# Tile offsets, parameter loads, scan outputs and two products in turn: one change in a four-part kernel

## The chip, the cores and the metric

The kernel runs on one core of a Trainium2 chip. The metric is device time in microseconds (us) per execution, the median of several runs. A profile is one further execution, recorded by the hardware profiler. Its spans are measured from the first to the last instruction of that execution.

## The reference

The input `x` has 512 tokens of width 1024, in fp32. Four mixers follow each other, each on a normalised copy of the residual `h`, and each adds its result to `h`:

```python
h = h + gated_delta_and_pool_mixer(rms_norm(h)) @ w_out              # first block
u = rms_norm(h); h = h + square(relu(u @ w_up)) @ w_down             # MLP, 1024 -> 4096 -> 1024
h = rms_norm(h)
h = h + nsa(rms_norm(h))     # attention: compressed, selected and window keys, gates, 16 heads of 64
h = h + s5(rms_norm(h))      # state space layer
return rms_norm(h)

# s5:
u, z = split(rms_norm(h) @ w_in, 2)                  # 2 x 1024 channels
y = scan(a, bb @ u) with (c_re, c_im) + d * u        # 64 groups of 16 channels, 64 complex states each
y = gelu(y)
ga, gb = split(y @ w_glu, 2)
out = (ga * sigmoid(gb) * silu(z)) @ w_out
```

The parameters of the scan come from `log_dt`, `lambda_re`, `lambda_im`, `b`, `c`: exponentials, sines and some 250 small elementwise operations on 128 x 64 tiles, and then tables of powers.

## The kernel before

Channels lie on the 128 partitions and the 512 tokens in the free dimension, so each of `h`'s 8 tiles is 128 x 512. Every large product is made in fp32 by three matmuls in a reduced format: a tile is split into `hi` (a rounded copy, made by ScalarE, ACT in the profile) and `lo` (the rest, made by VectorE, DVE), and a column block of a product adds up, for each of 8 input tiles, hi x hi, hi x lo and lo x hi: 24 matmuls with 512 columns. The input tiles' halves are `xhbuf` and `xlbuf`; the weights' raw tile is loaded by the queue of SyncE (SP), and its halves are `hi<-raw` (L103) and `lo<-raw,hi` (L104).

`Kit.jobs` is a list of weight tiles, in the order in which TensorE (PE) is to use them. `Kit.steps` goes through it and yields once for each matmul; a job may carry a `ready` function, and PE's program goes to something else until it is true. Raw tiles are fetched up to three jobs ahead and cut into halves one job ahead, each into one of two buffers. `Job.cut = (2, 7)` makes the products of two jobs alternate, input tile by input tile. `Kit.lead` emits a norm beside the first matmuls after it: the input tiles don't need the norm's factor, which is multiplied in when a product is taken out of PSUM; `first` and `second` count the matmuls before and after the sums of squares.

The stages of the profiled execution, in us: the first block up to about 309, the MLP to 693, the attention (nsa) to 1046, the S5 layer to 1356. In the S5 layer the scan runs from about 1091 to 1201, the gated product (glu) from 1205 to 1296, the last product to 1344.

Four places matter for the change.

*The parameters of the scan* (`Prepared.steps`, L1583). This is a generator that the MLP drives: after each `yield n` the MLP runs n matmuls. All loads of parameters are issued by GpSimd's queue (POOL in the profile), and all small operations are emitted before the MLP's first matmul, at a priority so low that the scheduler puts them wherever an engine has room. `FIRST = 480` matmuls later a loop over eight blocks begins; each makes its tables `F` and `V` on POOL (`matrices`, `times`: products of 128 x 1024 and 128 x 1152 elements) and writes them to DRAM. `matrices(0)` stands behind that first `yield`, but nothing in its priority holds it there.

*The attention's output product* (`QS` x `n_wout`, L130). Heads are worked in two halves, gp 0 and gp 1. The last output tile `og` of gp 0 is split into `QS` (ACT the copy, DVE the rest), and from then on the jobs of gp 0's half of the product are ready; they are fill for the softmax work of gp 1.

*The S5 input.* The first product of the S5 layer runs through its 8 input tiles in order, while the last of these are still being split from `h` (`xhbuf` L234, `xlbuf` L235).

*The scan and its outputs* (`S5.run`). For each of 8 blocks b: `u` goes to DRAM (`D<-u`) and comes back in another layout (`Uc<-D`), Toeplitz tables come back (`T<-DK`, from the queues of SP and ACT), `made<-DM` from POOL's queue, the products `pw`, `py` follow, and the result goes to DRAM (`yt`, `yc`, `D<-yc`). Between them PE works on the input products of `u` and `z`. All engines work here in the order in which the program is written (`manual_schedule`). Only when all that is emitted, `outputs(b)` loads each result back (`y<-D`), takes the gelu (its function table is loaded just before, L1944) and splits it into `xhbuf` and `xlbuf`, whose last use was the product of `z`. The glu product is ready when all 8 are emitted.

Memory on the right side of SBUF is allocated as a stack. `hpi` (128 x 1), `cm` (128 x 2 x 4) and `nc1` (128 x 648) have rows of 4, 32 and 2592 bytes, so that tiles allocated behind them (the attention's `QS`, `K`, `KL`, `Vt`, `P`, the scan's `keep`, the S5 layer's `szs`) start 32 bytes past a multiple of 64.

## Time and profile before

| | |
|---|---|
| median of 3 runs | 1361.2 us (1360.36 to 1363.26) |
| profiled execution: its own time | 1357.94 us |
| its span | 1356.2 us |
| mean granted clock of TensorE | 0.985 |
| busy in the span | PE 95%, weight loads 77%, DVE 69%, ACT 41%, POOL 29% |
| matmuls | 8360 |
| moved by DMA | 152.94 MB in 80877 packets |

PE's 95% leaves 69 us of the span in which it does nothing. An idle time of PE is told as the time before the instruction that ends it, with the instruction that it waited for. The page's slices show where PE ran at a lower granted clock.

### The profile page before, as it was taken

How to read it: one execution, taken by the hardware profiler on the slowest of the kernel's cores; microseconds unless marked ns; L12 is line 12 of the kernel's file. 1: busy time of each engine (PE TensorE's matmuls, PEld its weight loads, DVE VectorE, ACT ScalarE, POOL GpSimd, SP SyncE). 2: the span in 40 equal slices, each digit the busy share in tenths (PEclk: the TensorE clock that was granted, in tenths of full speed). 3: DMA queues.
4: the chain of work that ended last, by engine and by line, in shares of the span. 5: the costliest groups of instructions: out<-in, count | busy, mean ns of one | idle time of the engine just before them, and what ended most of it. 6: DMA issues, size and time to landing. Idle time of an engine off the chain costs nothing.

```text
span 1356.2 us, 22477 instructions
## 1 busy us (share of the span) xinstructions
PE 1287.1 (95%) x8360; PEld 1037.6 (77%) x8360; DVE 938.2 (69%) x2163; ACT 549.4 (41%) x1167; POOL 396.2 (29%) x412
## 2 busy tenths in 40 slices
PE   8799989999889999999999999998999999989997
PEld 5677766877668888788888777887777777768896
DVE  7977785699954767858676567876786665533465
ACT  4333232343222333233434555664764512254364
POOL 4722442221410455543121003443453200003200
PEclk8999999999989999999999999999999999989998
DMA  5110011252123443345435755312014379653231
GB/s 191 34 62 32 32 48 29 70 167 80 63 93 95 141 158 127 129 156 172 140 113 171 198 163 143 80 62 78 17 32 160 93 201 287 196 123 109 93 109 63
DMA packets 80877, 152.94 MB, mean 113 GB/s; under 512 B 23712, under 2 KB 45648, under 8 KB 79616
## 3 DMA queue, kind: packets, MB, share of 16 engines
q1 hardware_dynamic: 70832, 128.70, 31.1%
q0 software_dynamic: 2944, 17.50, 3.9%
q10 hardware_dynamic: 6992, 5.30, 1.4%
q8 instruction: 66, 1.08, 0.3%
q14 instruction: 43, 0.35, 0.1%
HBM read 119.60 MB, written 21.40 MB: 104 GB/s over the span
## 4 chain that ended last, share of the span: by engine, by line
PE 69%; DVE 17%; DMA 4%; issue 4%; ACT 3%; POOL 2%; SPq 1%; DVEq 0%; ACTq 0%; POOLq 0%
PE ps L130 48%; DVE lo L104 4%; PE ps L1865 3%; PE pa L1204 3%; PE acc L1299 2%; PE pt L1262 2%; DMA Uc<-D 2%; PE pv L1085 2%; DMA T<-DK 1%; DVE xlbuf L235 1%; ACT P L1213 1%; DVE r L377 1%; PE pb L576 1%; DVE cacc L454 1%; PE hid L1117 1%
## 5 line engine op out<-in xcount | busy, mean ns | idle before, releaser
L130 PE MATMUL ps<-xlbuf,hi 128*128 128x512 f32 x864 | 351.5, 407 | 6.3 <-DVE xlbuf L235 6.3
L130 PE MATMUL ps<-xhbuf,hi 128*128 128x512 f32 x864 | 349.9, 405 | 5.8 <-ACT xhbuf L232 4.0
L130 PE MATMUL ps<-xhbuf,lo 128*128 128x512 f32 x864 | 349.0, 404 | 0.1
L103 ACT CAST hi<-raw 128x512 fp32r<-128x512 f32 x357 | 203.5, 613 | 324.1 <-PE ps L130 233.4
L104 DVE TENSOR_TENSOR lo<-raw,hi 128x512 fp32r<-128x512 f32 x357 | 285.6, 824 | 69.0 <-ACT hi L103 66.0
L130 PEld LDWEIGHTS ps<-xhbuf,hi 128*128 128x128 f32 x864 | 163.7, 190 | 45.8 <-issue 6.7
L130 PEld LDWEIGHTS ps<-xlbuf,hi 128*128 128x128 f32 x864 | 164.1, 190 | 42.5 <-DVE xlbuf L235 9.0
L130 PEld LDWEIGHTS ps<-xhbuf,lo 128*128 128x128 f32 x864 | 164.1, 190 | 35.4 <-issue 4.5
L1218 POOL TENSOR_TENSOR P<-P,sm 128x128 f32<-128x128 f32 (+3 forms) x128 | 96.5, 775 | 199.2 <-DVE sm L1216 139.3
L130 PE MATMUL ps<-hh,lo 128*128 128x512 f32 x256 | 101.9, 398 | 6.1 <-DVE lo L104 6.1
L130 PE MATMUL ps<-hh,hi 128*128 128x512 f32 x256 | 100.9, 394 | 5.3 <-ACT hi L103 5.3
L130 PE MATMUL ps<-hl,hi 128*128 128x512 f32 x256 | 100.6, 393 | 0.1
L1213 ACT ACTIVATE P<-P,nm 128x128 f32<-128x128 f32 (+3 forms) x128 | 71.9, 563 | 61.3 <-DVE nm L1212 54.8
L1626 POOL TENSOR_TENSOR F<-keep 128x1024 f32<-128x1024 f32 x16 | 36.6, 2285 | 125.2 <-PE pt L1652 109.1
L1212 DVE CUSTOM_DVE_ANT_0 P<-pa,nc 128x128 f32<-128x128 f32 (+3 forms) x128 | 60.1, 484 | 13.1 <-PE pa L1204 12.6
L130 PEld LDWEIGHTS ps<-hh,lo 128*128 128x128 f32 x256 | 48.4, 189 | 19.1 <-DVE lo L104 8.8
L130 PEld LDWEIGHTS ps<-hh,hi 128*128 128x128 f32 x256 | 48.6, 190 | 15.8 <-ACT hi L103 6.1
L130 PEld LDWEIGHTS ps<-hl,hi 128*128 128x128 f32 x256 | 48.6, 190 | 10.8 <-DVE hl L232 0.6
L386 DVE TENSOR_TENSOR hbuf<-hbuf,ps 128x512 f32<-128x512 f32 x32 | 21.9, 685 | 48.1 <-PE ps L130 48.1
L1626 POOL TENSOR_TENSOR V<-keep 128x1152 f32<-128x1152 f32 x16 | 39.9, 2498 | 43.4 <-DMA DM<-V 42.8
L130 PE MATMUL ps<-QS,hi 128*128 128x512 f32 x128 | 47.6, 430 | 3.0 <-ACT QS L232 2.6
L1262 PE MATMUL pt<-ident,P 128*128 128x128 f32 x320 | 47.0, 275 | 3.5 <-ACT T L1266 1.9
(555 smaller groups left out, 2339.3 us busy)
## 6 DMA issues: line engine op xcount, KB each, us to landing
raw<-in_wup_dram SPq DMA_DIRECT2D x32, 512.0 KB, 3.5
raw<-in_wdown_dram SPq DMA_DIRECT2D x32, 512.0 KB, 3.6
made<-DM POOLq DMA_DIRECT2D x8, 1472.0 KB, 9.7
raw<-in_win_dram SPq DMA_DIRECT2D x19, 512.0 KB, 3.5
raw<-in_s_wglu_dram SPq DMA_DIRECT2D x16, 512.0 KB, 3.5
DM<-V SPq DMA_DIRECT2D x8, 576.0 KB, 3.1
DM<-Wt SPq DMA_DIRECT2D x8, 512.0 KB, 2.9
raw<-in_n_kv_dram SPq DMA_DIRECT2D x8, 512.0 KB, 3.9
```

Source lines behind the costliest of these rows:

```text
L103: self.nc.scalar.copy(hi[:, s], raw[:, s])
L104: self.nc.vector.tensor_tensor(lo[:, s], raw[:, s], hi[:, s].bitcast(F32), ALU.subtract)
L130: mm(ps, w[:, s], xs[k][x], start=k == 0 and n == 0, stop=k == kt - 1 and n == 2)
L1085: mm(R["v"][i], x[k][:, i * 128:i * 128 + 128], w[:, s], start=k == 0 and n == 0, stop=k == 7 and n == 2)
L1204: mm(pa[g2][:, 0:lead + nk], QS[gp][:, g2, i, r, :], keys[b][:, gp * 2 + g2, key0:AT[b] + nk], start=n == 0, stop=n == 1)
L1212: v.tensor_tensor_reduce(P[g2][:, 0:nk], pa[g2][:, lead:lead + nk], pos[:, 512 - nk:512], -slope, 3e38, ALU.add, ALU.min, nm[:, g2:g2 + 1])
L1213: act.activation(P[g2][:, 0:nk], P[g2][:, 0:nk], AF.Exp, scale=-1.0, bias=nm[:, g2:g2 + 1], accum_out=sm[:, g2:g2 + 1])
L1218: p.tensor_tensor(P[g2][:, 0:nk], P[g2][:, 0:nk], sm[:, g2:g2 + 1].to_broadcast([128, nk]), ALU.mult)
L1262: nc.tensor.transpose(pt[:, s], P[g2][:, s], ident)
L1299: mm(o[halves[g2], q * 128:q * 128 + 128], Vt[:, j, c:c + 64], T[g2][:, s], start=fresh and (q, j) == (0, 0), stop=(b, q, j) == (1, 3, i), ...
L1626: eng.tensor_tensor(o, self.S[f][:, js, b * 8:b * 8 + 8].rearrange("p j x -> p x j")[:, :, :, None].to_broadcast([128, 8, n, 16]), m[:, :, ...
L1865: nc.tensor.matmul(banks[m][:, 0:256], w[:, s], os[k][x][:, a * 256:a * 256 + 256], start=k == 0 and n == 0, stop=k == 7 and n == 2)
```

## The change

1. A tile of 32 bytes (`pad`) is allocated first on the right side; `hpi` and `cm` get 16 columns and `nc1` 656, so that the tiles named above start at multiples of 64 bytes.
2. `Job.whole`: where it is set, two jobs in turn do 21 matmuls of the first product, 21 of the second, and then the last input tile of each. The first two S5 input products are such a pair. `LEAD = 36, 34` takes the place of 28, 28, and `SPARE` falls from 60 to 46, so that as many matmuls come before the scan as before.
3. The parameters' loads go to SP's queue: three behind the first weights of the MLP (`NORM = 20` matmuls after the lead), the large one (`bc`, 1.5 MB) 300 matmuls later, together with the operations that use it (`last`) and `matrices(0)`. The loop over blocks begins at matmul 490 instead of 480.
4. `times` and the sums in `matrices` run as two halves each.
5. The jobs of gp 0's output product become ready when the second pair of heads of gp 1's first tile has been weighed (`seen.add(("out", 0))`), a few units later than before.
6. `outputs` is parted: `back(b)` loads the scan's result one block after it was computed, and `outputs(b)` takes gelu and split two blocks after, into tiles of their own (`yh`, `yl`). The tiles of the last product's input go into `K.xs` instead of into new ones. The last two `outputs` come behind `K.run(TAIL)`.

```diff
         self.consts = ctx.enter_context(tc.tile_pool(name="consts", bufs=1))
+        ctx.enter_context(tc.tile_pool(name="pad", bufs=1, side="right")).tile([128, 8], F32, name="pad")
...
-                for k in list(range(last)) + [None]:
-                    for n in range(count):
-                        for _ in range(3 if k is not None else 3 * (8 - last)):
-                            yield next(turns[n])
...
+                order = [(3 * last, n) for n in range(count)] if job.whole else [(3, n) for k in range(last) for n in range(count)]
+                for at, (some, n) in enumerate(order + [(3 * (8 - last), n) for n in range(count)]):
+                    for _ in range(some):
+                        yield next(turns[n])
...
-            K.queue(src, [add(m), add(m + 1)], lambda: ("o", gp) in seen)
+            K.queue(src, [add(m), add(m + 1)], lambda: ("out", gp) in seen)
...
+            if (gp, i, b, r) == (1, 0, 0, 1):
+                seen.add(("out", 0))
...
-                    seen.add(("o", gp))
+                    seen.add(("o" if gp == 0 else "out", gp))
...
-FIRST, EACH = 480, 60
-SPARE = 60
+FIRST, EACH = 490, 60
+NORM, BACK = 20, 170
+LEAD = 36, 34
+SPARE = 46
...
+            yield NORM
...
-                nc.gpsimd.dma_start(sc, consts)
-                nc.gpsimd.dma_start(self.dsk, W["dsk"])
+                nc.sync.dma_start(sc, consts)
+                nc.sync.dma_start(self.dsk, W["dsk"])
...
-                s5_params(K, P, W, sc, keep)
+                last = s5_params(K, P, W, sc, keep)
                 nc.gpsimd.dma_start(self.rho, S["rho"])
+            yield FIRST - BACK - NORM
+            with tc.high_priority(-LATER):
+                last()
+            temps.close()
...
-            yield FIRST
             F, Vt = self.matrices(0)
+            yield BACK
...
-        eng.tensor_tensor(o, self.S[f][:, js, b * 8:b * 8 + 8].rearrange("p j x -> p x j")[:, :, :, None].to_broadcast([128, 8, n, 16]),
-                          m[:, :, None, :].to_broadcast([128, 8, n, 16]), ALU.mult)
+        for x in (0, 4):
+            eng.tensor_tensor(o[:, x:x + 4], self.S[f][:, js, b * 8 + x:b * 8 + x + 4].rearrange("p j x -> p x j")[:, :, :, None].to_broadcast([128, 4, n, 16]),
+                              m[:, x:x + 4, None, :].to_broadcast([128, 4, n, 16]), ALU.mult)
...
-        p.tensor_tensor(F, F, F2[:, :, 0:8], ALU.add)
+        for x in (slice(0, 4), slice(4, 8)):
+            p.tensor_tensor(F[:, x], F[:, x], F2[:, x, 0:8], ALU.add)
...
+        yh, yl = (szp.tile([128, 8, 512], F32R, name=n) for n in ("yh", "yl"))
...
-                oh = so.tile([128, 512], F32R, name=f"oh{m}", bufs=1)
-                ol = so.tile([128, 512], F32R, name=f"ol{m}", bufs=1)
+                oh, ol = K.xs[m]
...
+        def back(b):
+
+            y = got[b] = K.work.tile([128, 512], F32, tag="sq", name="sq")
+            nc.sync.dma_start(y.rearrange("p (j n) -> p j n", j=8), self.D2[b].rearrange("(j c) (g n) -> (c g) j n", j=8, n=64))
+
         def outputs(b):
 
-            y = self.sw.tile([128, 512], F32, tag="u", name="y", bufs=3)
-            nc.sync.dma_start(y.rearrange("p (j n) -> p j n", j=8), self.D2[b].rearrange("(j c) (g n) -> (c g) j n", j=8, n=64))
+            y = got.pop(b)
             nc.scalar.activation(y, y, AF.Gelu_apprx_tanh)
-            K.split(*K.xs[b], y)
-            ys.append(K.xs[b])
+            K.split(yh[:, b, :], yl[:, b, :], y)
+            ys.append((yh[:, b, :], yl[:, b, :]))
+
+        first[0].cut, first[0].whole = (2, 7), True
...
-            K.lead(K.norm_steps(wcol, R, permute=True), R, held)
+            K.lead(K.norm_steps(wcol, R, permute=True), R, held, *LEAD)
...
                     K.run(n)
-            K.run()
-            for b in range(8):
-                outputs(b)
+                if b > 0:
+                    back(b - 1)
+                if b > 1:
+                    outputs(b - 2)
+            back(7)
+            K.run(TAIL)
+            outputs(6)
+            outputs(7)
```

How the engines' programs change at three places. The first is the MLP's beginning. DVE's program before, in the MLP's first nine column blocks, when the last parameters are worked out (`t`, `r` and `hl` belong to the blocks, `lo` to the weights, the rest to the parameters):

```order
L1447 TENSOR_TENSOR bct<-bcraw,cis 128x1024
L1447 TENSOR_TENSOR keep<-keep,bct 128x8x128
L375 TENSOR_TENSOR t<-ps,rstd 128x512
L104 TENSOR_TENSOR lo<-raw,hi 128x512
L377 SCALAR_TENSOR_TENSOR r<-t 128x512
L104 TENSOR_TENSOR lo<-raw,hi 128x512
L1682 TENSOR_TENSOR f_4353<-sc,keep 128x256
L232 TENSOR_TENSOR hl_3666<-r,hh_3665 128x512
L1683 TENSOR_TENSOR f_4354<-sc,keep 128x256
L1569 TENSOR_SCALAR keep<-keep 128x8x64
L1684 TENSOR_TENSOR rd<-f_4353,f_4354 128x256
```

and POOL's program behind it, the tables of blocks 0 and 1:

```order
L1606 DMA rhos<-keep 128x64
L1626 TENSOR_TENSOR F<-keep 128x1024
L1626 TENSOR_TENSOR V<-keep 128x1152 x2
L1626 TENSOR_TENSOR F_4205<-keep 128x8x128
L1638 TENSOR_TENSOR F<-F,F_4205 128x1024
L1626 TENSOR_TENSOR V_4210<-keep 128x1152
L1643 TENSOR_TENSOR V<-V,V_4210 128x1152
```

The same nine blocks in DVE's program now, around one of them:

```order
L1514 TENSOR_SCALAR ser<-ser 128x64
L1484 SCALAR_TENSOR_TENSOR s<-thh,s 128x64
L1454 TENSOR_TENSOR f<-f,k 128x64
L1513 SCALAR_TENSOR_TENSOR ser<-ser,aa 128x64
L1454 TENSOR_TENSOR t_3266<-f,s 128x64
L377 TENSOR_TENSOR t<-ps,rstd 128x512
L1492 TENSOR_SCALAR keep<-t_3266 128x64
L1514 TENSOR_SCALAR ser<-ser 128x64
L379 SCALAR_TENSOR_TENSOR r<-t 128x512
L1493 TENSOR_SCALAR keep<-keep 128x64
L106 TENSOR_TENSOR lo<-raw,hi 128x512 x2
L234 TENSOR_TENSOR hl_3612<-r,hh_3611 128x512
```

and POOL's tables now:

```order
L1619 DMA rhos<-keep 128x64
L1644 TENSOR_TENSOR F<-keep 128x512 x2
L1644 TENSOR_TENSOR F_3944<-keep 128x4x128 x2
L1657 TENSOR_TENSOR F<-F,F_3944 128x512 x2
L1644 TENSOR_TENSOR V<-keep 128x576
L1644 TENSOR_TENSOR V_3952<-keep 128x576 x2
L1644 TENSOR_TENSOR V<-keep 128x576
L1663 TENSOR_TENSOR V<-V,V_3952 128x576 x2
```

The early small operations (`ser`, `thh`, `xbr` and the like) now stand where the late ones stood: from the third `hl` to the first `hbuf` of the down product there are 13, 12, 20, 23, 20, 22 and 19 of them between two rows of these names, 129 in all. The ones on `bcraw` and `bct` have moved into the first down product, around its seventh column block, and POOL's tables behind them. A table is made in halves.

The second place is PE's program in the attention, at gp 0's last weighing (`acc<-T,Vt` x16; `pt` are the transposes of the probabilities, `pa` the scores). Before:

```order
L1299 MATMUL acc<-T,Vt 64x128 x16
L130 MATMUL ps<-QS_6268,hi 128x512 x2
L130 MATMUL ps<-QS_6268,lo 128x512
L1262 MATMUL pt<-ident,P 128x128 x2
L130 MATMUL ps<-QS_6268,hi 128x512 x2
L1204 MATMUL pa<-K_6271,QS_6269 128x128
L1204 MATMUL pa<-KL_6273,QS_6269 128x128
```

Now:

```order
L1303 MATMUL acc<-T,Vt 64x128 x16
L1264 MATMUL pt<-ident,P 128x128 x2
L1206 MATMUL pa<-K_6323,QS_6321 128x128
L1206 MATMUL pa<-KL_6325,QS_6321 128x128
L1206 MATMUL pa<-K_6323,QS_6321 128x128
L1206 MATMUL pa<-KL_6325,QS_6321 128x128
L1264 MATMUL pt<-ident,P 128x128 x2
L1303 MATMUL acc<-T,Vt 64x128 x4
L132 MATMUL ps<-QS_6320,hi 128x512
```

The first product on the new `QS` comes behind two transposes, four scores, two more transposes and four weighings, which stood behind it.

The third place is SP's queue in the scan, when `Uc` of blocks 4 and 5 is loaded. Before:

```order
L212 DMA D_10777<-u 128x8x64
L1824 DMA Uc<-D_10775 128x512
L1741 DMA T<-DK_2987 16x8x128 x4
L97 DMA raw<-in_s_wz_dram 128x1024
L212 DMA D_10778<-u 128x8x64
L1824 DMA Uc<-D_10776 128x512
L1741 DMA T<-DK_2988 16x8x128 x4
```

Now (D_10831 and D_10832 are the results of blocks 0 and 1):

```order
L214 DMA D_10829<-u 128x8x64
L1964 DMA sq<-D_10831 128x8x64
L1846 DMA Uc<-D_10827 128x512
L1761 DMA T<-DK_2991 16x8x128 x4
L99 DMA raw<-in_s_wz_dram 128x1024
L214 DMA D_10830<-u 128x8x64
L1964 DMA sq<-D_10832 128x8x64
L1846 DMA Uc<-D_10828 128x512
L1761 DMA T<-DK_2992 16x8x128 x4
```

Each result's load `sq<-D` stands ahead of the `Uc` of a block four later. ACT's program gets the gelu (`sq<-sq`) ahead of the copy `yt` of a block two later.

## Rows read from the trace of the kernel before

**Rows 1.** The page's part 1: busy us, share of the span, instructions, by engine.

```profile
PE 1287.1 (95%) x8360; PEld 1037.6 (77%) x8360; DVE 938.2 (69%) x2163; ACT 549.4 (41%) x1167; POOL 396.2 (29%) x412
```

**Rows 2.** Windows: us, length, busy by engine (instructions), granted clock, DMA share, GB/s.

```profile
320.00:350.00 30.00, 30.00 (x132) 24.50 (x131) 29.73 (x96) 10.13 (x18) 0.58 (x1) 1.00 0.27 89
350.00:380.00 30.00, 20.06 (x85) 15.26 (x83) 29.06 (x27) 5.38 (x11) 20.40 (x8) 0.96 0.18 53
380.00:444.00 64.00, 63.66 (x272) 52.52 (x273) 31.30 (x53) 17.63 (x32) 0.00 (x0) 0.96 0.31 99
1070.00:1090.00 20.00, 19.30 (x76) 14.91 (x77) 10.18 (x24) 4.01 (x7) 0.00 (x0) 0.91 0.42 122
1142.00:1155.00 13.00, 13.00 (x125) 10.20 (x126) 9.14 (x15) 3.32 (x7) 0.53 (x1) 1.00 1.02 260
1205.00:1250.00 45.00, 44.46 (x182) 35.56 (x183) 19.51 (x28) 22.81 (x39) 9.33 (x7) 0.94 0.40 112
```

**Rows 3.** The page's part 5: the down products' matmuls; busy, mean ns, idle before.

```profile
L130 PE MATMUL ps<-hh,lo 128*128 128x512 f32 x256 | 101.9, 398 | 6.1 <-DVE lo L104 6.1
L130 PE MATMUL ps<-hh,hi 128*128 128x512 f32 x256 | 100.9, 394 | 5.3 <-ACT hi L103 5.3
```

**Rows 4.** Timeline of DVE: start, duration (us), line, operation; 272 to 360.

```profile
277.34 0.23 DVE L1406 SCALAR_TENSOR_TENSOR dt<-dt,xar 128x64 f32<-128x64 f32 x1
...
333.72 0.69 DVE L232 TENSOR_TENSOR hl<-r,hh 128x512 fp32r<-128x512 f32 x1
...
339.31 0.69 DVE L232 TENSOR_TENSOR hl<-r,hh 128x512 fp32r<-128x512 f32 x1
...
359.78 2.76 DVE L104 TENSOR_TENSOR lo<-raw,hi 128x512 fp32r<-128x512 f32 x1
```

**Rows 5.** Timeline of POOL over the same stretch.

```profile
354.61 2.03 POOL L1626 TENSOR_TENSOR F<-keep 128x1024 f32<-128x1024 f32 x1 [13.33 <-DVE keep L1447]
356.60 5.39 POOL L1626 TENSOR_TENSOR V<-keep 128x1152 f32<-128x1152 f32 x2
```

**Rows 6.** Timelines of PE, DVE and POOL in the attention, 938 to 945.

```profile
943.79 0.49 PE L130 MATMUL ps<-QS,hi 128*128 128x512 f32 x1 [2.56 <-ACT QS L232]
944.69 0.80 PE L130 MATMUL ps<-QS,hi 128*128 128x512 f32 x1 [0.40 <-DVE QS L232]
...
943.07 0.15 DVE L1216 TENSOR_TENSOR sm<-sm,G 128x2 f32<-128x2 f32 x1
...
943.40 1.50 POOL L1218 TENSOR_TENSOR P<-P,sm 128x128 f32<-128x128 f32 x2 [3.48 <-DVE sm L1216]
```

**Rows 7.** Timelines of PE and DVE at the S5 layer's beginning.

```profile
1069.49 0.50 PE L130 MATMUL ps<-xhbuf,hi 128*128 128x512 f32 x1 [1.73 <-ACT xhbuf L234]
1070.70 0.79 PE L130 MATMUL ps<-xlbuf,hi 128*128 128x512 f32 x1 [0.70 <-DVE xlbuf L235]
...
1068.09 1.28 DVE L104 TENSOR_TENSOR lo<-raw,hi 128x512 fp32r<-128x512 f32 x2
```

**Rows 8.** Chain of waits in the scan (start, us, what), and PE's timeline.

```profile
1133.15 11.43 DMA Uc<-D
1144.61 11.00 DMA T<-DK
...
1157.42 11.87 DMA Uc<-D
...
1171.93 0.66 PE L1807 MATMUL py<-ident,yt 128*128 128x128 f32 x4 [0.94 <-ACT yt L1799]
```

**Rows 9.** Timelines of PE and ACT where the glu product begins.

```profile
1205.54 0.80 PE L130 MATMUL ps<-xhbuf,hi 128*128 128x512 f32 x1 [3.97 <-ACT xhbuf L232]
...
1202.54 1.28 ACT L1944 ACT_TABLE_LOAD   x1
```

**Rows 10.** Groups of PE's weight loads by form: busy us, mean ns, idle before.

```profile
L1262 PEld LDWEIGHTS pt<-ident,P 128*128 128x128 f32 x320 | 38.3, 140 | 12.9 <-POOL P L1218 3.1 <-issue 3.0 <-POOL sc L1250 0.2
...
L1652 PEld LDWEIGHTS pt<-ident,F 128*128 128x128 f32 x64 | 7.5, 141 | 1.0
```

More of the change, by code (lines that the diff above doesn't have):

```diff
@@ L59, with __init__ @@
 class Job:
-    def __init__(self, src, width, products=None, ready=None, cut=None, store=None):
-        self.src, self.width, self.products, self.ready, self.cut, self.store = src, width, products, ready, cut, store
+    def __init__(self, src, width, products=None, ready=None, cut=None, store=None, whole=False):
+        self.src, self.width, self.products, self.ready, self.cut, self.store, self.whole = src, width, products, ready, cut, store, whole
 class Kit:
@@ L177, in steps @@
                 self.fetch(t + count)
-                for k in list(range(last)) + [None]:
-                    for n in range(count):
-                        for _ in range(3 if k is not None else 3 * (8 - last)):
-                            yield next(turns[n])
-                        if k is None and n == 0:
-                            halves[t] = raws[t] = None
-                            self.cut(t + count)
+                order = [(3 * last, n) for n in range(count)] if job.whole else [(3, n) for k in range(last) for n in range(count)]
+                for at, (some, n) in enumerate(order + [(3 * (8 - last), n) for n in range(count)]):
+                    for _ in range(some):
+                        yield next(turns[n])
+                    if at == len(order):
+                        halves[t] = raws[t] = None
+                        self.cut(t + count)
                 for n in range(1, count):
@@ L1593, in steps @@
             self.dsk = keep_p.tile([128, 16], F32, name="dsk")
-            self.hp = keep_p.tile([128, 1], F32, name="hpi")
+            self.hp = keep_p.tile([128, 16], F32, name="hpi")[:, 0:1]
             keep = keep_p.tile([128, KEPT_W], F32, name="keep")
             self.S = S = kept(keep)
-            with tc.high_priority(-LATER), tc.tile_pool(name="spt", bufs=1, side="right") as P:
-                nc.gpsimd.dma_start(sc, consts)
-                nc.gpsimd.dma_start(self.dsk, W["dsk"])
+            temps = ExitStack()
+            P = temps.enter_context(tc.tile_pool(name="spt", bufs=1, side="right"))
+            with tc.high_priority(-LATER):
+                nc.sync.dma_start(sc, consts)
+                nc.sync.dma_start(self.dsk, W["dsk"])
                 zero = P.tile([128, 224], F32, name="zero").rearrange("p (h n) -> p h n", h=2)
@@ L1642, in matrices @@
         self.times(p, V, "pr", rc[:, 0:8], 9, b)
-        p.tensor_tensor(V, V, V2, ALU.add)
+        for x in (slice(0, 4), slice(4, 8)):
+            p.tensor_tensor(V[:, x], V[:, x], V2[:, x], ALU.add)
         return F, V
@@ L1983, in run @@
             steps = 8 * 4 - 1
-            left = 384 - 56 - SPARE - TAIL
+            left = 384 - sum(LEAD) - SPARE - TAIL
             for b in range(8):
```

43 lines of the change are left out of this document (23 added, 20 removed).

## The prediction

> **What bounds the kernel now.** I read the page's busy shares first: PE works 95% of the span [rows 1], so the time can only fall by PE's idle time (69 us) and by the time in which its clock was low. Then I listed PE's idle times with what ended them, and asked for windows over each of the stretches that the change touches. Two adjoining windows show what to look for. From 320 to 350 us PE is never idle: 132 matmuls in 30.00 us, 0.2273 us each, at a granted clock of 1.00. From 350 to 380 it does 85 [rows 2]. The reader is to see that a stretch has a normal price per matmul, and that what it takes beyond that is what an edit there can win. Outside the stretches below the change leaves PE's work and its waits alone; the first block has many waits, but they belong to the delta net.
>
> **The MLP's beginning.** 350 to 380 takes 30.00 - 85 x 0.2273 = 10.7 us too long, and 380 to 444, at clock 0.96, takes 64.00 - 272 x 0.2273 = 2.2 us too long [rows 2]: 12.9 us, of which 10.3 is idle time (30.00 - 20.06 and 64.00 - 63.66) and the rest a clock that fell in it. Over the whole MLP the down products waited 6.1 + 5.3 = 11.4 us for halves of weights [rows 3], so 1.1 of these lie elsewhere. The halves were late because DVE's part of them took 2.76 us at 359.78 against the 0.69 of an undisturbed operation of that size [rows 4], while POOL did tables of 2.03 and 2.7 us without a pause [rows 5]; a DVE operation that meets one ends with it.
>
> The change takes the tables of block 0 away from there: `matrices(0)` now begins after matmul 320, in the down product, whose column blocks have one DVE operation and two `lo` each, where the up products have five. In the tables' old place stand small parameter operations. Can DVE carry them? From one `hl` to the next (333.72 to 339.31) it ran 18 small operations and five large ones in 5.59 us [rows 4]; PE needs 24 x 0.2273 = 5.46 for the same block. The new order has 129 small ones in seven intervals, 18.4 each. At that rate DVE falls behind by about 7 x 0.13 + 3 x 0.15 = 1.4 us over all of them, and the weights are cut a block ahead, so no wait. If each small operation had to wait for the one before, as in the chain at 277 us (0.23 each [rows 4]), it would be 129 x 0.23 + 35 x 0.69 - 7 x 5.46 = 15.6 us late: that is the other bound, and the orders shown interleave three chains, so I take the first. Then POOL's tables meet the second up product, with halves half as long. I leave 1.4 us for that. Gain 11.5 us, bounds 0 and 12.9. The halves may also remove the 1.1 elsewhere; I take 0.5. The loads that change queues end nothing here: 1.5 MB ahead of one weight tile is 5.8 us at the 260 GB/s that the scan reaches [rows 2], and weights are fetched up to three blocks of 5.46 us ahead.
>
> **The attention.** PE waits 2.56 + 0.40 us for `QS` [rows 6]. The new order puts two transposes, four scores and two more transposes ahead of it. But the second pair of transposes needs probabilities that POOL multiplied from 943.40 to 944.90, after DVE's `sm` at 943.07 [rows 6]. PE reaches them about 0.7 us after the weighing, at 942, so it waits there instead, for about as long; in DVE's program that `sm` has even moved behind two scores. So one wait takes the other's place: 0, bounds -1 and +3.
>
> **The S5 input.** PE waits 1.73 us for the last `xhbuf` and 0.70 for the last `xlbuf` [rows 7], and 1070 to 1090 runs at 0.91 [rows 2]: 20 x 0.09 = 1.8 us, 4.2 in all. With 21 matmuls of the second product in between, the last tile is needed 4.8 us later and is there. But the second product needs its own `lo`, which DVE makes from 1068.09 to 1069.37 [rows 7], behind the last sum into `h`, and both orders have it there. PE would be at that matmul at 1068.0 and wait about 1 us (1.28 / 2 and the way). I take 2.5, bounds 0 and 4.2.
>
> **The scan.** Here the change adds something. From 1142 to 1155 the DMA engines are full (share 1.02, 260 GB/s), while PE is never idle [rows 2]. The chain of waits runs over transfers alone from 1133 to 1169 (`Uc` 11.43, `T` 11.00, `Uc` 11.87) and comes out at PE once, as 0.94 us before the transposes of block 5 [rows 8]. Each `sq<-D` brings 0.26 MB, 1.0 us at 260 GB/s, and stands in SP's queue ahead of `Uc` and four `T`; in ACT's program the gelu stands ahead of `yt`, of `T`'s issues and of `hi`. Four results are loaded before 1171, so the wait there grows by up to 4 us. If the queues have more slack than the chain shows, it is 0; if every load also delays the ACT work behind its gelu, three times that. I take -4, bounds 0 and -12.
>
> The Trainium skill's page "DMA: Bandwidth & Descriptors" (Specifications) speaks against this part more than my price does: below 512 B a transfer doesn't reach line rate, since the engine reads, changes and writes back. The rows of these loads have 256 B; by that rule they would cost perhaps twice their bytes (my estimate from the page), -8, and the forecast would be 1348. `Uc` has the same rows and lands in 11.43 to 11.87 us here [rows 8], but no run here shows what part of that is its rows.
>
> **The glu's beginning.** PE waits 3.97 us for the first split, behind a table load of 1.28 us on ACT [rows 9], and then runs at 0.94: 182 matmuls in 45 us [rows 2] are 3.1 us beyond the price, when the 0.54 us of the wait inside the window is left out; 7.1 in all. Now six of eight tiles are split before the scan ends; the last two follow the last z product. The first two glu products go in turn, six matmuls per input tile, so that the seventh tile is needed 36 x 0.2273 = 8.2 us after the start. ACT and DVE need about 2.5 us for the two. Gain 6.5, bounds 3 and 7.1. Late next would be the second glu weight, behind the last `sq` in SP's queue, but it has the same time.
>
> **The padding** I cost at nothing. Tiles off a 64-byte boundary (`P`) load as weights in 140 ns, tiles on one (`F`) in 141 [rows 10]; bounds 0 and 3 us.
>
> **The sum.** 11.5 + 0.5 + 0 + 2.5 - 4 + 6.5 = 17.0 us. The profiled execution took 1357.94 us (span 1356.2), so 1340.9; it lies 3.3 us below the median of the runs, and on the median's scale the forecast is 1344.2 us.
>
> **Rivals.**
> *All that shows goes.* 12.9 + 1.1 + 3.0 + 4.2 + 7.1 = 28.3 us, and the scan hides its loads: 1333. For it: the loads fall into a stretch in which PE is never idle. Against it: the DMA engines are full there and the chain already ends at PE.
> *The MLP's wait moves.* The small chains are serial, or POOL's tables meet the up product as they did before; the gain there is 2 instead of 12: 1354. For it: DVE is busy 29.73 of 30 us in the stretch where the work goes [rows 2]. Against it: the same density ran there without a wait.
> *Slower: the scan is paced by its transfers.* Each block's `yt` stands behind a gelu that waits for a load issued a block earlier. The block's period is 12.1 us (from the two `Uc` issues, 24.3 us for two [rows 8]), and a load lands in about 11.9, so from there on every us of landing is a us of PE, in five blocks (0 to 4). The gains elsewhere are 21 us, so it decides from landings of 11.9 + 4.2 = 16.1 us; at 17 the loss is 25.5 and the time 1366. For it: the share of 1.02. Against it: 8% more bytes (0.26 of 13 x 0.26 = 3.4 MB) make 12.8 of 11.9, not 16.
> *It does nothing*: each wait is replaced where it stood, as in the attention.
>
> **How the numbers follow.** The forecast's case has a chance of 0.62 (1338 to 1350 by its own bounds), all goes 0.12, the MLP's wait moves 0.14, slower scan 0.08, nothing 0.04. The range of 1333 to 1356 leaves out the slow case, the case of nothing and half of the better one's lower side. A measurement of this kernel can tell 0.2% (2.7 us) from no change. Faster by more: 0.62 + 0.12 + 0.14 less 0.02 for its upper end, 0.86; within: 0.05; slower: 0.09.
>
> **What would show it.** In the profile after: the down products' idle time below 2 us in place of 11.4, and a clock of 1.00 from 350 to 440 (MLP); a wait for POOL's `P` of 2 to 4 us in place of the one for `QS` (attention); about 1 us before `lo` in the second S5 product; waits of 2 to 5 us in sum before `yt`, with landings of `sq` of 10 to 13 us (scan); no wait over 1 us and a clock of 1.00 at the glu's beginning. The prediction is wrong if DVE's lateness in the first up product stops PE, if `yt` waits in each block, or if products on the padded tiles get cheaper.

## The result

The changed kernel takes 1348.63 us (median of 4 runs, 1347.37 to 1349.54) beside 1361.19 before (1360.36 to 1363.26): a ratio of 0.9905, 95% interval 0.9888 to 0.9922. That is 12.6 us faster; 17.0 were forecast. The time lies 4.4 us above the forecast of 1344.2 and inside the range. The profiled execution was the slowest of the four, 1349.54 us, so the two profiles are only 8.4 us apart (1357.94 and 1349.54). One execution of a later kernel, both_behind, took 6706.7 us, which nothing here explains; its ratio leaves it out.

PE's share rose by one point; POOL has 44 instructions more (the halves). Part 1 of the changed kernel's page, to be read beside [rows 1]:

```profile
span 1347.4 us, 22525 instructions
PE 1289.7 (96%) x8360; PEld 1041.2 (77%) x8360; DVE 934.4 (69%) x2163; ACT 548.1 (41%) x1167; POOL 414.5 (31%) x456
```

The windows of the changed kernel (columns as in [rows 2]) show where to look. The sixth line lies inside the gated product (glu); the seventh is the same stretch of the kernel before:

```profile
350.00:380.00 30.00, 30.00 (x134) 24.85 (x133) 29.35 (x141) 8.09 (x14) 0.57 (x1) 1.00 0.33 107
400.00:430.00 30.00, 23.86 (x92) 18.51 (x91) 28.87 (x31) 7.35 (x15) 22.83 (x16) 0.89 0.15 46
1110.00:1150.00 40.00, 37.85 (x354) 29.52 (x352) 24.72 (x39) 13.58 (x24) 1.59 (x3) 1.00 0.96 276
1150.00:1180.00 30.00, 26.64 (x235) 20.72 (x234) 16.95 (x28) 7.97 (x14) 0.00 (x0) 0.94 0.77 204
1197.00:1242.00 45.00, 44.14 (x188) 34.86 (x187) 16.34 (x24) 15.71 (x27) 9.34 (x7) 1.00 0.30 97
1217.00:1282.00 65.00, 65.00 (x281) 52.72 (x280) 28.10 (x40) 24.98 (x45) 15.29 (x12) 1.00 0.32 97
1225.00:1290.00 65.00, 65.00 (x289) 53.83 (x288) 27.96 (x39) 25.02 (x45) 16.77 (x14) 1.00 0.31 97
```

350 to 380 is repaired: 134 matmuls at full clock in place of 85, with 141 DVE operations beside them. But 400 to 430 is a new hole: 92 matmuls where 134 have room, at clock 0.89, and POOL's tables are there. In the scan PE is idle for 2.2 + 3.4 us from 1110 to 1180. The glu's beginning is at full clock now, but behind it, with PE never idle and the clock full in both kernels, 65 us hold 281 matmuls in place of 289.

PE's timeline names the waits behind this (start, duration, operation, idle time before it and its releaser). Changed kernel, in the MLP, the attention, the S5 input, the scan and the glu:

```profile
413.85 0.50 PE L132 MATMUL ps<-xhbuf,hi 128*128 128x512 f32 x1 [2.71 <-ACT hi L105]
415.58 0.80 PE L132 MATMUL ps<-xhbuf,lo 128*128 128x512 f32 x1 [0.97 <-DVE lo L106]
426.39 0.50 PE L132 MATMUL ps<-xhbuf,lo 128*128 128x512 f32 x1 [2.46 <-DVE lo L106]
934.35 0.66 PE L1303 MATMUL acc<-T,Vt 128*64 128x128 f32 x8 [0.66 <-DVE og L1309]
937.01 0.69 PE L1264 MATMUL pt<-ident,P 128*128 128x128 f32 x2 [0.78 <-POOL P L1220]
1073.09 0.73 PE L132 MATMUL ps<-xhbuf,hi 128*128 128x512 f32 x1 [0.94 <-DVE u L1851]
1128.79 1.09 PE L1810 MATMUL py<-T,Uc 128*64 128x128 f32 x16 [0.95 <-DMA T<-DK]
1149.49 0.66 PE L1827 MATMUL py<-ident,yt 128*128 128x128 f32 x4 [1.20 <-ACT yt L1819]
1165.49 1.11 PE L1827 MATMUL py<-ident,yt 128*128 128x128 f32 x4 [3.37 <-ACT yt L1819]
1198.21 0.50 PE L132 MATMUL ps<-yh,hi 128*128 128x512 f32 x1 [0.86 <-ACT hi L105]
```

None of the waits of [rows 3, 6, 7, 9] is left where it was; each line above is a new one. The down products wait for nothing (the page's part 5 has 0.0 us where [rows 3] have 6.1 and 5.3).

To price the parts I cut each profile at PE's first or last matmul of a stage. Lengths in us, one profile per kernel; the columns after the second belong to the experiments below:

| stage | before | after | scan undone | gelu behind | phases behind | both behind | phases, no scan | key undone | queue undone | halves undone |
|---|---|---|---|---|---|---|---|---|---|---|
| output product, first block | 48.4 | 45.1 | 45.0 | 45.1 | 45.1 | 45.1 | 45.1 | 45.0 | 48.5 | 45.1 |
| MLP | 383.0 | 375.6 | 377.2 | 377.2 | 367.2 | 367.2 | 367.2 | 375.6 | 379.7 | 383.6 |
| attention's QS products, first to last | 119.1 | 116.3 | 116.4 | 116.3 | 117.9 | 116.2 | 116.4 | 119.1 | 115.8 | 116.3 |
| S5 input | 34.1 | 34.4 | 32.5 | 33.7 | 32.6 | 32.6 | 33.0 | 32.7 | 32.4 | 32.1 |
| scan | 97.1 | 103.4 | 96.0 | 100.0 | 103.8 | 96.9 | 95.8 | 104.3 | 101.7 | 102.6 |
| glu | 101.8 | 98.3 | 102.0 | 99.1 | 98.0 | 98.9 | 102.1 | 98.3 | 98.0 | 98.0 |

Before to after: 3.4 + 7.3 + 2.8 - 0.3 - 6.3 + 3.5 = 10.4 us won here. One profile is one execution: the MLP of this code takes 375.6 us in one further profile (key undone) and 377.2 to 377.3 in five (two in the table, and loads_pool, lead_undone and pad_undone), where the clock falls a second time, at 426 or soon after, so 7.3 may be 5.8. The first block ahead of these stages, which the change leaves alone, took 258.8 us in this profile and 256.2 in the one before (clock 0.89 beside 0.97 from 40 to 100), and 256.1 to 260.5 in the experiments: that part of the difference between the profiles is not the change's.

### The profile page after: what moved, and what is told of

Read it like the earlier page. It is cut to its first block, busy times and chain, and to the rows that moved or that the text cites. A ratio compares the mean times of both kernels' runs of the same rounds, so it can differ in the third digit from the quotient of the medians.

```text
span 1347.4 us, 22525 instructions
## 1 busy us (share of the span) xinstructions
PE 1289.7 (96%) x8360; PEld 1041.2 (77%) x8360; DVE 934.4 (69%) x2163; ACT 548.1 (41%) x1167; POOL 414.5 (31%) x456
## 4 chain that ended last, share of the span: by engine, by line
PE 75%; DVE 13%; issue 3%; DMA 3%; ACT 3%; POOL 2%; SPq 0%; DVEq 0%; ACTq 0%; POOLq 0%
PE ps L132 53%; PE ps L1886 3%; DVE lo L106 3%; PE pa L1206 3%; PE acc L1303 2%; PE pt L1264 2%; PE pv L1087 2%; DMA T<-DK 1%; DVE xlbuf L237 1%; ACT P L1215 1%; PE pb L578 1%; PE hid L1119 1%; DMA sq<-D 1%; PE py L1817 1%; PE pu L587 1%
## 5 line engine op out<-in xcount | busy, mean ns | idle before, releaser
L132 PE MATMUL ps<-xlbuf,hi 128*128 128x512 f32 x736 | 302.9, 412 | 4.4 <-DVE xlbuf L237 4.3
L132 PE MATMUL ps<-xhbuf,hi 128*128 128x512 f32 x736 | 301.9, 410 | 3.7 <-ACT hi L105 2.7
L132 PE MATMUL ps<-xhbuf,lo 128*128 128x512 f32 x736 | 299.1, 406 | 4.3 <-DVE lo L106 4.3
L132 PEld LDWEIGHTS ps<-xhbuf,hi 128*128 128x128 f32 x736 | 140.4, 191 | 38.5 <-issue 5.1
L132 PEld LDWEIGHTS ps<-xhbuf,lo 128*128 128x128 f32 x736 | 140.9, 191 | 35.4 <-DVE lo L106 6.7
L132 PEld LDWEIGHTS ps<-xlbuf,hi 128*128 128x128 f32 x736 | 140.2, 190 | 35.5 <-DVE xlbuf L237 7.2
L1644 POOL TENSOR_TENSOR F<-keep 128x512 f32<-128x512 f32 x32 | 42.0, 1334 | 80.7 <-PE pt L1672 50.4
L1644 POOL TENSOR_TENSOR V<-keep 128x576 f32<-128x576 f32 x32 | 45.3, 1436 | 35.9 <-DMA DM<-V 35.4
L132 PE MATMUL ps<-yh,hi 128*128 128x512 f32 x128 | 50.6, 396 | 0.9 <-ACT hi L105 0.9
L132 PE MATMUL ps<-yh,lo 128*128 128x512 f32 x128 | 50.7, 396 | 0.0
```

Source lines behind the costliest of these rows:

```text
L132: mm(ps, w[:, s], xs[k][x], start=k == 0 and n == 0, stop=k == kt - 1 and n == 2)
L1644: eng.tensor_tensor(o[:, x:x + 4], self.S[f][:, js, b * 8 + x:b * 8 + x + 4].rearrange("p j x -> p x j")[:, :, :, None].to_broadcast([128, ...
```

## The experiments

All are the changed kernel with the edit shown, timed in five rounds beside the kernel before on the same chip. They are compared by the ratio to before, which for the changed kernel is 0.9905 [0.9888, 0.9922]; 0.001 is 1.36 us. Where the intervals of two ratios overlap, the text says so.

### The MLP: what makes 400 to 430 late

DVE's timeline there, changed kernel:

```profile
400.90 2.44 DVE L106 TENSOR_TENSOR lo<-raw,hi 128x512 fp32r<-128x512 f32 x2
403.27 1.33 DVE L1702 TENSOR_TENSOR f<-sc,keep 128x256 f32<-128x256 f32 x1
...
411.34 1.19 DVE L1708 TENSOR_SCALAR f<-f 128x256 f32<-128x256 f32 x1
412.45 0.68 DVE L377 TENSOR_TENSOR t<-ps,rstd 128x512 f32<-128x512 f32 x1
413.83 1.70 DVE L106 TENSOR_TENSOR lo<-raw,hi 128x512 fp32r<-128x512 f32 x1 [0.70 <-ACT hi L105]
415.45 1.89 DVE L379 SCALAR_TENSOR_TENSOR r<-t 128x512 f32<-128x512 f32 x1
...
423.14 0.43 DVE L1704 TENSOR_TENSOR rd<-f,f 128x256 f32<-128x256 f32 x1
```

POOL's timeline of the same stretch:

```profile
399.45 6.12 POOL L1644 TENSOR_TENSOR F<-keep 128x512 f32<-128x512 f32 x4 [29.81 <-DVE keep L1454]
405.53 2.89 POOL L1657 TENSOR_TENSOR F<-F,F 128x512 f32<-128x512 f32 x2
408.39 5.21 POOL L1644 TENSOR_TENSOR V<-keep 128x576 f32<-128x576 f32 x4
```

ACT's timeline of the same stretch:

```profile
400.07 1.15 ACT L105 CAST hi<-raw 128x512 fp32r<-128x512 f32 x2 [4.30 <-PE ps L132]
412.56 0.42 ACT L1710 ACTIVATE f<-f 128x256 f32<-128x256 f32 x1 [11.35 <-DVE f L1708]
...
413.19 1.12 ACT L105 CAST hi<-raw 128x512 fp32r<-128x512 f32 x2
```

The seven `f` and `rd` operations belong to `phases(0)`, which the program issues only in the next down product; the scheduler brings them here, because their inputs are ready. Beside the tables each takes about as long as one table operation (1.2 to 1.4 us beside 1.3 to 1.6; `rd` at 423.14, after the tables, 0.43). On ACT the abs (L1710) that waits for the last of them stands ahead of two `hi`, 11.35 us. So PE waits for `hi`, then for `lo`.

**phases_behind** queues them behind the last DVE operation of the MLP that has been issued:

```diff
-nc.sync.dma_start(self.D[b][:, 2176:MADE], self.phases(b)...)
+with tc.issue_after(K.last.ins):        # last hl or sum into h
+    C = self.phases(b)
+nc.sync.dma_start(self.D[b][:, 2176:MADE], C...)
```

> Only DVE's order in the MLP is changed: the phase operations of block 0 and 1 (14 of 1.3 us beside POOL's tables at 403 to 423) are held back to the place where the program issues them, in the next down product, after POOL's tables of block 0. Theory (the waits of 2.71, 0.97 and 2.46 us at 411 to 424 come from DVE and POOL together, because DVE has the phases beside lo and r): most of the 6.1 us and the low clock behind them (20 us at 0.83, about 2 us) go: 1341 to 1344. Rival (POOL's tables alone make lo and r late, at 1.7 to 1.9 us each instead of 0.7): the waits stay in the up product, 1347 to 1349.

Measured: 1340.62 us (1338.88 to 1341.04), ratio 0.9846 [0.9824, 0.9869], 8.0 us below the changed kernel. The window of this kernel:

```profile
400.00:430.00 30.00, 30.00 (x134) 24.86 (x133) 27.52 (x27) 9.01 (x16) 24.67 (x16) 1.00 0.26 82
```

All 134 matmuls fit, though POOL is as busy as before the edit and the operations that meet it are as slow. DVE's timeline, same kernel:

```profile
405.53 0.69 DVE L377 TENSOR_TENSOR t<-ps,rstd 128x512 f32<-128x512 f32 x1 [2.39 <-PE ps L132]
406.14 0.84 DVE L106 TENSOR_TENSOR lo<-raw,hi 128x512 fp32r<-128x512 f32 x1
406.90 1.78 DVE L379 SCALAR_TENSOR_TENSOR r<-t 128x512 f32<-128x512 f32 x1
```

So the rival (tables alone make PE wait) is wrong: DVE can carry the slowed `lo`, `r` and `hl`, but not the phases as well. The edit takes the abs out of ACT's way together with the phases; no run parts the two.

**halves_undone** takes back the halving of POOL's tables:

```diff
-for x in (0, 4):
-    eng.tensor_tensor(o[:, x:x + 4], ...[128, 4, n, 16], ALU.mult)
+eng.tensor_tensor(o, ...[128, 8, n, 16], ALU.mult)          # and F + F2, V + V2 whole
```

> Only the halving of POOL's tables is undone (whole operations of 1024 and 1152 elements in place of two halves each). Theory (my term: halves are worth 0.5 us outside the first block): 1349.1 within 1. Rival (a DVE operation that meets a table ends with it, so with whole tables of 2.0 to 2.8 us the lo, r and f of 411 to 424 take up to 2.8 us each in place of 1.3 to 1.9): the waits of 6.1 us there grow by 3 us or more, 1352.

Measured: 1353.96 us (1351.35 to 1355.6), ratio 0.9945 [0.9927, 0.9962]: 5 us lost, on the rival's side and beyond its 1352. DVE's timeline of this kernel:

```profile
400.52 4.30 DVE L106 TENSOR_TENSOR lo<-raw,hi 128x512 fp32r<-128x512 f32 x2
404.74 2.48 DVE L1699 TENSOR_TENSOR f<-sc,keep 128x256 f32<-128x256 f32 x1
...
417.27 2.13 DVE L1704 TENSOR_TENSOR f<-f,f 128x256 f32<-128x256 f32 x1
419.43 0.29 DVE L1705 TENSOR_SCALAR f<-f 128x256 f32<-128x256 f32 x1
```

and the wait of PE that it ends in:

```profile
421.04 0.80 PE L132 MATMUL ps<-xhbuf,hi 128*128 128x512 f32 x1 [10.28 <-ACT hi L105]
```

A 128x256 operation now takes 2.1 to 2.8 us, one whole table each, and 0.29 as soon as the tables are over. PE's one wait is 10.28 us. The MLP takes 383.6 us, as long as before the change: without halves, and with the phases where they are, moving the tables would have won nothing there.

**param_queue** takes back only the queue of four parameter loads:

```diff
-nc.sync.dma_start(raw, W["par"])       # and bc, consts, dsk
+nc.gpsimd.dma_start(raw, W["par"])
```

> Only the queue of four parameter loads is undone (par, bc, consts, dsk on POOL's queue, as before the change); the points at which the program issues them stay. The order on SP and PE is the program's; on DVE, ACT and POOL it is the scheduler's, which issues early what is ready early. Theory (the queue holds the parameter operations in their new place, since a load in SP's queue comes at its place in the program): DVE's parameter operations stand in the output product and at the MLP's beginning again, POOL's tables of block 0 meet the first down product: the waits of 10.3 us at 360 to 380 come back, and 3.4 us before the MLP; the 6.1 us at 411 to 424 and their low clock (2 us) go: 1348.6 + 10.3 + 3.4 - 8.1 = 1354. Rival (the points of issue hold them): 1348.6 within 1.5.

Measured: 1352.04 us (1351.6 to 1357.7), ratio 0.9941 [0.9921, 0.9962]: 3.4 us lost by the medians, 4.9 by the ratios, whose intervals just touch. The output product is back at 48.5 us, and the waits for `lo` and `hi` are back in the first down product, while 400 to 430 is free of them. PE's timeline of this kernel:

```profile
370.17 0.79 PE L132 MATMUL ps<-hh,lo 128*128 128x512 f32 x1 [3.88 <-DVE lo L106]
...
382.12 0.50 PE L132 MATMUL ps<-hh,hi 128*128 128x512 f32 x1 [4.02 <-ACT hi L105]
```

The queue holds the parameters in their place: a load in SP's queue comes where the program has it, and what needs it can't be brought forward. The points of issue alone hold nothing on DVE and POOL.

### The scan: order on ACT, or transfers

ACT's timeline in the changed kernel:

```profile
1157.92 1.14 ACT L105 CAST hi<-raw 128x512 fp32r<-128x512 f32 x2 [7.14 <-DMA T<-DK]
1162.46 0.63 ACT L1969 ACTIVATE sq<-sq 128x512 f32<-128x512 f32 x1 [3.41 <-DMA sq<-D]
...
1164.86 0.58 ACT L1819 COPY yt<-py 128x512 f32<-128x512 f32 x1
```

ACT's timeline in both_behind (below), where the gelu comes after `yt` and the issue of its write:

```profile
1148.39 0.58 ACT L1821 COPY yt<-py 128x512 f32<-128x512 f32 x1
...
1151.02 0.55 ACTq L1832 DMA_DIRECT2D D<-yc  x1
1151.61 0.63 ACT L1971 ACTIVATE sq<-sq 128x512 f32<-128x512 f32 x1 [1.07 <-issue]
```

In the first, the gelu of an older batch stands ahead of `yt` and waits 3.41 us for its load; PE's 3.37 us at 1165.49 is that wait. The first three loads of `sq`, in the full stretch, land in 9.6 to 11.7 us, less than the 16.1 from which my slower rival decides.

**gelu_behind** changes ACT's order alone:

```diff
+self.sent = nc.scalar.dma_start(self.D2[b], yc...)
 if b > 1:
-    outputs(b - 2)
+    with tc.issue_after(self.sent.ins):
+        outputs(b - 2)
```

> All loads as in the changed kernel; only on ACT each gelu now stands behind the batch's yt, yc and the issue of its write, in place of ahead of yt. Theory A (ACT's order: yt stands behind a gelu that waits for its load): the waits before the transposes of yt (1.20 at 1148, 3.37 at 1162) go, 3 to 4.5 us: 1344 to 1345.6. Rival B (the transfers, or SP's queue, pace the batch, whichever order ACT has): a wait for T or Uc takes their place, 1348.6 within 1.5 us.

Measured: 1343.43 us (1342.17 to 1346.68), ratio 0.9874 [0.9852, 0.9896], 5.2 us below the changed kernel by the medians, 4.2 by the ratios, whose intervals overlap a little; both_behind below repeats the gain clear of noise. Theory A: the waits for `yt` are gone. In the profiled execution, the slowest of the six (1346.68 us), another wait stands in the scan:

```profile
1144.15 1.09 PE L1810 MATMUL py<-T,Uc 128*64 128x128 f32 x16 [2.56 <-DMA D<-yc]
```

This product reads `T` and `Uc`, and a DMA ended its wait (the profile names that of `yc`, which the product doesn't read). So B, the transfers, has a share in this execution.

**loads_pool** changes the queue alone:

```diff
-nc.sync.dma_start(y..., self.D2[b]...)
+nc.gpsimd.dma_start(y..., self.D2[b]...)
```

> Only the queue of the eight loads of scan results is changed: POOL issues them in place of SP, so that Uc and T no longer stand behind them. Theory A (ACT's order): the sq loads have the same transfers and the gelu the same place; if a load is issued about as early, 1348.6 within 1.5; only the load that SP issued at 1155.27, behind T's, comes up to 5 us earlier, and then the 3.37 us at 1162 go: 1345. Rival B (DMA engines full, share 0.96): nothing lands earlier, and the z weights or T take the delay: 1348 to 1350. Rival C: POOL's queue waits for the write of yc and holds back the load of the next made tile behind it: slower, 1350 or more.

Measured: 1349.69 us (1347.11 to 1354.3), ratio 0.9922 [0.9896, 0.9948]: no gain, which is rival B's figure. A wait for `yt` is still there, 2.51 us at 1162.34, but not behind a gelu: the gelu of that place is done at 1155.68, and ACT's timeline has

```profile
1161.10 0.56 ACTq L1761 DMA_DIRECT2D T<-DK  x1
1161.70 0.59 ACT L1819 COPY yt<-py 128x512 f32<-128x512 f32 x1 [4.03 <-DMA T<-DK]
```

Here `yt` stands in ACT's order behind the issue of a load of `T`, which waits for the landing of an earlier one. So freeing SP's queue of the eight loads isn't enough, and a gelu is not the only thing on ACT that can hold `yt`.

**scan_undone** takes the scan's part back:

```diff
-    back(b - 1); outputs(b - 2)            # in each batch, into yh, yl
+K.run()                                    # all z products
+for b in range(8): back(b); outputs(b)     # into K.xs; oh, ol in tiles of their own
```

> Only the scan's part of the change is undone: the eight results are loaded, passed through the gelu and split after the last z product, into the tiles of the S5 input, as before the change. Theory (loads and gelus cost the scan more than they give the glu): in the two profiled executions the scan grew by 6.3 us (first pw to last yt) and the glu's beginning shrank by 3.5, so undoing gives 2.8 us back: about 1345.8, with the yt wait of 3.37 us at 1162 gone and a wait of some 4 us before the first glu product in its place. Rival 1 (my terms, -4 and +6.5): undoing loses 2.5 us, 1351.1. Rival 2 (the scan's growth is a disturbance of one profile): undoing loses the 3.5 to 6.5 us of the glu, 1352 to 1355.

Measured: 1346.04 us (1342.18 to 1349.89), ratio 0.9890 [0.9866, 0.9914], 2.6 us below the changed kernel, as the theory had it, though the intervals overlap and so don't show it. By the table the scan gets 7.4 us back and the glu loses 3.7 (its wait is 3.98 us again).

**both_behind**: phases_behind and gelu_behind together.

> The two reorderings together: DVE's phase operations behind POOL's tables in the MLP (alone 1340.6, 8.0 us below the changed kernel), ACT's gelus behind yt, yc and its write in the scan (alone 1343.4, 5.2 below). Theory (two separate waits of two stages): the gains add up, 1348.6 - 8.0 - 5.2 = 1335.4. Rival (the scan is paced by transfers, and the 5.2 us are the luck of where T lands): 1338 to 1341, with a wait for T of 2 to 4 us in the scan.

Measured: 1333.34 us as the median of all six executions, 1332.87 as that of the five between 1332.49 and 1334.22; ratio of these five 0.9792 [0.9774, 0.9809]. It is 15.3 to 15.8 us below the changed kernel, 2 to 3 better than the sum of the two edits, which is within the noise. It beats the kernel before, the changed kernel and phases_behind by more than the intervals, so moving the gelus is worth about 7 us there (1340.62 less 1333.34). The scan takes 96.9 us.

**phases_no_scan**: phases_behind and scan_undone together.

> DVE's phase operations behind POOL's tables (as in the run at 1340.6), and the scan's part of the change undone. It measures what that part is worth with ACT's order put right, without the noise of the MLP: beside the run with both reorderings (1333.3). Theory (the loads cost the scan about 1 us, the gelu's place in ACT's order the rest of the 6 to 7): the part is worth the glu's 3.5 less 1, and this run takes 1336 to 1338. Rival (the scan's part loses 2.6 us whatever the order, as scan_undone and the changed kernel measured, and the gain of the two reorderings has another cause): 1331 to 1333.

Measured: 1336.11 us (1335.37 to 1336.99), ratio 0.9814 [0.9794, 0.9833], about 3 us above both_behind; the ratios' intervals overlap a little, but the slowest of that kernel's five (1334.22) is faster than the fastest of this one. So, once ACT's order is right, the scan's part is worth having: in these two profiles the loads cost the scan 96.9 - 95.8 = 1.1 us, and the glu wins 102.1 - 98.9 = 3.2.

**weight_ahead_t**: both_behind, and in SP's queue each load behind the next batch's `Uc` and `T`, the second glu weight ahead of the last load.

```diff
-if b > 0: back(b - 1)                       # at a batch's end
+if at == 0 and b > 1: back(b - 2)           # behind the next batch's T
-back(7); K.run(TAIL)
+back(6); K.run(1); back(7); K.run(TAIL - 1)
```

> Both reorderings (1333.3) and two moves in SP's queue: each load of a scan result behind the next batch's Uc and T instead of ahead of them, and the second glu weight ahead of the last such load. Theory (T's wait of 0.94 us at 1117 and the wait of 1.41 us for the second weight's hi at 1180 come from that queue): both go, 1331. Rival (the loads only delay something else by as much: the last gelus come later, and the seventh and eighth glu input are late): 1333.3 within 1, with a wait for yh or yl in the glu.

Measured: 1333.22 us (1331.86 to 1335.48), ratio 0.9794 [0.9774, 0.9815]: the same, not the 1331 of the theory. The glu's wait of 1.41 us and the one for `T` (0.94) went, but `yt` waits 0.79 us once more: not worth the edit.

### The small terms

**key_undone**:

```diff
-if (gp, i, b, r) == (1, 0, 0, 1): seen.add(("out", 0))
-seen.add(("o" if gp == 0 else "out", gp))
+seen.add(("out", gp)); seen.add(("o", gp))
```

> Only the early start of the attention's output product is undone: it is ready after og again, as before the change, and the transposes and scores stand behind it. Theory by the two traces (first to last QS product 2.79 us shorter, the way to the first 0.69): 3.5 us are lost, 1352.1, with waits of 2.6 and 0.4 us for QS in place of 0.66 and 0.78. Rival (my term: POOL's P takes the place of QS, 0): 1348.6 within 1.

Measured: 1350.98 us (1349.07 to 1353.11), ratio 0.9922 [0.9905, 0.9938]: 2.3 us lost by the medians and by the ratios, though the intervals overlap. PE's timeline of this kernel has the old waits [rows 6] again, to a hundredth:

```profile
932.25 0.49 PE L132 MATMUL ps<-QS,hi 128*128 128x512 f32 x1 [2.57 <-ACT QS L234]
933.15 0.50 PE L132 MATMUL ps<-QS,hi 128*128 128x512 f32 x1 [0.40 <-DVE QS L234]
```

**lead_undone**:

```diff
-LEAD, SPARE = (36, 34), 46;  first[0].cut, first[0].whole = (2, 7), True
+LEAD, SPARE = (28, 28), 60
```

> Only the S5 input's beginning is undone: the first two products one after the other, 28 and 28 matmuls ahead of the norm's sums and of its factor (now 36 and 34), 60 ahead of the scan (now 46). Rival (my term): 2.5 us are lost, 1351.1, with the waits of 1.7 and 0.7 us for xhbuf and xlbuf back. Theory by the traces (from the last QS product to the first pw the changed kernel took 0.33 us more: the waits went, but PE waits 0.94 us for a bank that u, behind the later factor, holds, and its clock was 0.91): nothing is lost, 1348.6 within 1.5, without the wait of 0.94 us.

Measured: 1348.2 us (1347.01 to 1350.51), ratio 0.9902 [0.9887, 0.9917]: the same. The old waits are back (1.62 and 0.69 us for `xhbuf` and `xlbuf`), and the 0.94 us for `u` is gone, as the theory had it.

**pad_undone**:

```diff
-ctx.enter_context(tc.tile_pool(name="pad", ...)).tile([128, 8], F32, name="pad")   # cm, hpi, nc1 as before
```

> Only the padding is undone: the 8 spare columns, cm, hpi and nc1 at their old sizes. Theory (my term): 0, 1348.6 within 1, and the weight loads of the tiles that the padding moves as long as before. Rival (a tile off a 64-byte boundary is slower to read): slower by up to 3 us, 1351.6, with PE's matmuls or weight loads longer over the whole span.

Measured: 1352.28 us (1346.85 to 1353.91), ratio 0.9925 [0.9905, 0.9946]. Its interval overlaps that of the changed kernel. PE's idle times of over 0.2 us add up to 49.9 us in both, and a weight load of the normalised tiles takes 192 ns beside 191; the profile is longer where its clock is lower, in the first block above all (260.5 us beside 258.8). One stretch shows a cost of the old addresses, inside the glu, to be read beside the sixth window above:

```profile
1221.00:1286.00 65.00, 65.00 (x279) 52.25 (x278) 27.72 (x40) 24.56 (x45) 15.30 (x12) 1.00 0.32 97
```

From start to start the glu's matmuls take 234 ns here on average and 232 in the ten other profiles that read `yh` and `yl`: 0.7 us in 384 matmuls. Whether the rest of the 2.7 us between the ratios is the padding's stays open.

## Why the prediction was right, and where it wasn't

The sum had the right sign and the time is in the range, but most of its terms were off, and the errors partly cancelled: that the total came so near is in part luck. Term by term, by the table:

- **MLP, 12.0 forecast, 7.3 measured.** Right: DVE carried the 129 small operations without stopping PE (no idle time from 350 to 400), and the old waits went. The step that failed is "POOL's tables meet the second up product ... I leave 1.4 us for that". It cost 375.6 - 367.2 = 8.4 us (8.0 timed). I looked for the operations that must stand beside the tables (`t`, `lo`, `r`, `hl`) and not for those that may: the phases became ready with the parameters, so the scheduler put them there. They were in DVE's order, ahead of the up product's `t`, `lo` and `r`. With them out of the way the MLP takes 367.2, a gain of 15.8, beyond my upper bound of 12.9 + 1.1: 0.8 us of the excess is a wait for `xlbuf` at the MLP's beginning (1.74 us before, 0.92 in phases_behind) that the bound left out; the rest stays open. The rival "the MLP's wait moves" happened, at half its size: 7.3 lies midway between its 2 and my 12.
- **Halves, 0.5 forecast, about 5 measured**, inside the MLP's term. [Rows 4, 5] had it: a DVE operation that meets a table ends shortly after it (359.78 + 2.76 = 362.54, the table 356.60 + 5.39 = 361.99). In a row of operations each one meets a table of its own, so the length of a table multiplies by their number.
- **Output product of the first block, 0 forecast, 3.4 measured.** The step that failed is "the first block has many waits, but they belong to the delta net": param_queue alone brings these 3.4 us back, so they were the parameters'. I gave nothing for the place that they left.
- **Attention, 0 forecast, 2.8 measured** (2.3 timed). The step that failed is "PE ... waits there instead, for about as long": the P that I named from [rows 6] was not the one that those transposes need. They ran without a wait; the P after them cost 0.78 us and `og` 0.66, 1.4 in place of 3.0. The rest goes with the clock, which I did not count: 0.89 from 938 to 953 before, 1.00 from 930 to 945 after.
- **S5 input, 2.5 forecast, -0.3 in the profile, 0 timed.** The waits of [rows 7] went, as said. What I did not see: the later norm factor lets `u` hold its PSUM bank longer (0.94 us; it goes in lead_undone). The wait of about 1 us before `lo` that I took off came as 0.45. The rest of this profile's loss is a clock of 0.86 from 1071 to 1083, which two other profiles of the same code at that place do not have (1.00); in the eight other columns with this input it takes 32.1 to 33.7.
- **Scan, -4 forecast, -6.3 measured.** Place and mechanism were right (the gelu ahead of `yt`). The size was a bound from landings, and "the wait there grows by up to 4 us" counted four loads of 1 us each; one gelu alone waited 3.41, because its load was issued late, at 1155.27, behind `T`. Besides the two waits for `yt` (1.20 and 3.37) there is one for `T`, 0.95, which the reordering leaves (0.94 in both_behind). The slower rival did not come: landings stayed below its 16.1 us.
- **Glu, 6.5 forecast, 3.5 measured.** The clock is 1.00 as said. "Late next would be the second glu weight ... but it has the same time" failed: it stood behind the last load and its `hi` cost PE 0.86 us. The greater loss is a term that I didn't have: the glu's matmuls became slower. In the kernel before, and in the two runs with the scan's part undone, they read `xhbuf` and `xlbuf` and follow each other every 227 ns; where they read the new tiles `yh` and `yl`, every 232, with PE never idle at full clock (289 and 281 matmuls in 65 us, above). Over 384 matmuls that is about 1.9 us. Every version with the long wait takes 101.8 to 102.1 us, every one without it 97.4 to 99.2.
- **Padding, 0 forecast**: about right. My sign of being wrong (products on padded tiles get cheaper) is there in the glu alone, 0.7 us by pad_undone; the run's time doesn't show it.

My estimate of 8 us for rows of 256 B, worked out from the Trainium skill's page "DMA: Bandwidth & Descriptors" (Specifications), comes near the 6.3 us for another reason. With the same loads and the gelu behind, the scan's loss is 1.1 us in the pair of profiles above (4.0 in the profile of gelu_behind, with its wait of 2.56 us). The loads do take long to land, but then little has to wait for them.

## What to carry to other kernels

When work is moved into a place with room, list also what becomes ready with it: an operation without a pinned place follows its inputs, and on an in-order engine it stands ahead of work that PE needs. Hold it back by what makes it ready (a load in an ordered queue) or by an explicit order on its engine. Where an engine does optional work with a late input, put that work behind the copies that PE waits for, not ahead. And where an input moves to a new tile, compare matmuls per us at full clock before and after: a stretch without idle time can still have become slower.
